# Mixer layer with 32 experts on one core: five expert weight loads ahead of the output projection instead of four, two buffers for normalized rows, gates times b2 at experts 6, 12, 18 and 24

## The chip, the core and the metric

The kernel runs on one core of one Trainium2 chip. The metric is the device time of one execution in microseconds (us). A core has five engines that run their own instruction queues: TensorE (PE in the rows; PEld is its weight load), VectorE (DVE), ScalarE (ACT), GpSimd (POOL) and SyncE (SP), whose queue here issues the weight loads. They wait for each other through semaphores. Transfers run on 16 DMA engines that all queues share.

## What is computed

One layer over 512 latent tokens of width 1024 (with 256 context tokens): an adaptive LayerNorm, one input projection whose columns feed a bidirectional RWKV-7 part and a Fourier part, one output projection, a residual with LayerNorm, then a mixture of experts and a second residual with LayerNorm. The change touches the seam between the output projection and the experts. Each token takes 4 of 32 experts; `gate` is the softmax over its four router logits. For the rows `u` of one expert `e`:

```
h   = u @ w1[e] + b1[e]            # 1024 -> 2 x 1024, two halves: linear and gated
act = clamped_swiglu(h)            # 1024
y   = act @ w2[e] + b2[e]          # 1024 -> 1024
out[token] += gate[token, e] * y   # scattered back, then the second residual and LayerNorm
```

The kernel adds the term `gate * b2` apart from the rest: for each group of 128 tokens, the matrix of gates (128 x 32) times `b2` (32 x 1024).

## The kernel before

**Output projection (L1553 to L1597).** Four tiles of 128 tokens go one after another. For each, TensorE makes the projection (L875, L914), VectorE takes mean and variance of it from PSUM (L1566, L1567) and writes the normalized rows to the tile `yo` (L1573); TensorE transposes them (L1578), ScalarE scales them (L1581), TensorE makes the router logits (L1584) and transposes back (L1591), VectorE adds the bias and takes the eight largest logits (L1585, L1586), ScalarE copies out the experts' input (L1592). GpSimd makes the residual from `yo` (L1595, L1596). The last L1586 is followed by the router (from L1627) and that by the experts. The rows that the projection reads are closed by a "finish" chain on VectorE, ScalarE and TensorE (L834, L836, L841, L844, L850, L852, L856, L857), once for each half of its columns.

**Expert constants.** Ahead of the four tiles in the program stand loads and preparations for the experts. The bias b1 comes in two tiles `b1r` of 1024 columns, which take the same tag `yo` and so the same buffers as the normalized rows. ScalarE makes a bf16 copy `b1s` (L1545), VectorE subtracts it (L1548), and ScalarE stores the rest as further bf16 parts (L1549). `b2r` is b2 times a modulation vector (L1551, GpSimd).

**Experts.** 32 experts, each with a fixed number of slots: 128, 32, 160, 32, 96, 64, 96, 192, 32, 64, 96, ... . The slots are cut into blocks of 64 and 32 rows. Expert i has 8 up slabs (w1) and 4 down slabs (w2), each a load of 1 MB on SP's queue (L1328, `raw<-in_w`), 384 loads in one stream, into 14 buffers: RAWA of them in a pool that is opened ahead of the projection, RAWB in one that is opened when the router's buffers are gone. A buffer comes free when TensorE has multiplied its slab with the expert's blocks (L1337). In step i of `all_experts` stand in this order: the slots of expert i+2 (one-hot products L1249, gather L1305), the up products of expert i (L1337, closed by the bias product L1344 with `sel`, which GpSimd casts at L1300), the transposes of the activations of expert i-1 (L1389) and of the rows of expert i+1 (L1316), the down products of expert i-1 (L1337 on `at`), VectorE's product with the gate (L1408) and the accumulate into DRAM (L1414, an indirect transfer from GpSimd's queue). One-hot products, transposes and the product below write to `pt`, two PSUM buffers in all.

**Gates times b2.** `b2_part(j)` treats the j-th 128 tokens: four matmuls (L1479), two copies of PSUM to the tile `yb` by ScalarE (L1480; `yb` has one buffer), and one accumulate of 512 KB on GpSimd's queue (L1481). Before, it is called in steps 4, 5, 6 and 7.

A recording layer gathers all instructions and a scheduler sets the order on each engine, so that program order is only a preference; each engine then runs its row strictly in order.

Of the kernel before, what the change touches and what calls it, by code (L numbers as in the profile page):

```python
# [10 lines left out]
F32 = mybir.dt.float32  # L11
# [9 lines left out]
T, TC, D = 512, 256, 1024  # L21
# [123 lines left out]
def body(ctx, tc, I, out, dbg=None, stop=None):  # L145
# [944 lines left out]
    P = Pair()  # L1090
    P.po = po
    post = moe(tc, I, ck, h2d, accd, modd, P)
    next(post)
    pq = pool(sO[1], "pq", side="right")
# [30 lines left out]
    sK.close()  # L1125


RAWA, RAWB = 4, 10
LATE = ("y64", "y32", "act64", "act32", "at64", "at32", "sg", "slin", "sth")
FIRST = 200  # L1130
NBLK = 48
# [56 lines left out]
def moe(tc, I, ck, h2d, accd, modd, P):  # L1188
# [6 lines left out]
    def pool(stack, name, bufs=1, **kw):  # L1195
        return stack.enter_context(tc.tile_pool(name=name, bufs=bufs, reuse_waits="tile", **kw))
# [269 lines left out]
    def place(i):  # L1466
        j, cap = PLAN[i]
        return Expert(cap, rm[:, :, j], R6[:, :, j], sel3[:, j:j + 1])

    def chosen(i):  # L1470
        j = PLAN[i][0]
        return SY.value_load(eidi[0:1, j:j + 1], min_val=0, max_val=NE - 1)

    def b2_part(j):

        y = B.tile([128, D], F32, "yb", 1)
        for n in range(2):
            p = pst.tile([128, 512], F32, name="pt", tag="pt")
            PE.matmul(p, gwT[:, j * 128:(j + 1) * 128], b2r[:, n * 512:(n + 1) * 512], start=True, stop=True)  # L1479
            A.activation(y[:, n * 512:(n + 1) * 512], p, AF.Copy)  # L1480
        G.indirect_dma_start(out=accd[:, :], out_offset=bass.IndirectOffsetOnAxis(ap=toki[:, j:j + 1], axis=0),  # L1481
                             in_=y, in_offset=None, compute_op=ALU.add)

    def all_experts():
        cur, prev = first, None
        ahead = [place(i) for i in range(1, len(PLAN))]
        yield cur.split
        yield ahead[0].fetch
        for i in range(len(PLAN)):
            nxt = ahead[i] if i + 1 < len(PLAN) else None  # L1490
            if i + 2 < len(PLAN):
                yield ahead[i + 1].fetch
            ups = list(cur.up())
            yield from ups[:8 if nxt else 4]
            if nxt:
                nxt.weights(chosen(i + 1))
            if prev:
                yield prev.turn
            if nxt:
                yield nxt.split  # L1500
            if prev:
                yield from prev.down()
                yield prev.put
                if 4 <= i < 8:
                    yield lambda j=i - 4: b2_part(j)
            if not nxt:
                yield from ups[4:]
            prev, cur = cur, nxt
        yield prev.turn
        yield from prev.down()  # L1510
        yield prev.put
# [4 lines left out]
    po = pool(so, "pl", side="left")  # L1516
# [9 lines left out]
    B = Buffers(None, 99, (praw, RAWA))  # L1526
    first = Expert(PLAN[0][1], rm0, R60, M["sel0"][0:96]).weights(0)
    experts = Run(all_experts())
    experts.load(RAWA)
    sb_ = ExitStack()  # L1530
# [8 lines left out]
            SY.dma_start(z[n * h:n * h + n], row_bcast(modd, 8 * n, 3072 + 8 * n * h, n))  # L1539
    for n in range(2):  # L1540
        c = slice(n * D, (n + 1) * D)
        b1r = po.tile([128, D], F32, name="yo", bufs=3)
        for h in range(3):
            SY.dma_start(b1r[32 * h:32 * h + 32], I["b1"][0][:, c])
        A.activation(b1s[:, c], b1r[0:96], AF.Copy)  # L1545
        for h in (1, 2, 2):
            q = slice(32 * h, 32 * h + 32)
            V.tensor_tensor(b1r[q], b1r[q], b1s[q, c], op=ALU.subtract)  # L1548
            A.activation(b1s[q, c], b1r[q], AF.Copy)  # L1549
# [5 lines left out]
    for j in P.order:  # L1555
        tk = slice(j * 128, (j + 1) * 128)
        p = mixer(j)
        if "y" in dbg:
            y = po.tile([128, D], F32, name="yd")
            for hh in range(2):  # L1560
                A.activation(y[:, hh * 512:(hh + 1) * 512], p[hh], AF.Copy)
            SY.dma_start(dbg["y"][tk, :], y)
        st = po.tile([128, 2, 6], F32, name="sto", bufs=2)
        mv = po.tile([128, 2], F32, name="mvo", bufs=2)
        for hh in range(2):
            V.bn_stats(st[:, hh, :], p[hh])  # L1566
        V.bn_aggr(mv, st)  # L1567
        rs = po.tile([128, 1], F32, name="rso", bufs=2)
        A.activation(rs, mv[:, 1:2], AF.Sqrt, bias=epsl, scale=1.0)
        V.reciprocal(rs, rs)  # L1570
        y = po.tile([128, D], F32, name="yo", bufs=3)
        for hh in range(2):
            V.tensor_scalar(y[:, hh * 512:(hh + 1) * 512], p[hh], mv[:, 0:1], rs, op0=ALU.subtract, op1=ALU.mult)  # L1573
        h2T = po.tile([128, KD, 128], F32, name="h2T", bufs=2)
        for q in range(2):
            pt = pst.tile([128, 4, 128], F32, name="pt")
            for z in range(4):
                PE.transpose(pt[:, z], y[:, (4 * q + z) * 128:(4 * q + z + 1) * 128], ident)  # L1578
            for z in range(4):
                k = 4 * q + z  # L1580
                A.activation(h2T[:, k], pt[:, z], AF.Identity, bias=B2c[:, k:k + 1], scale=G2c[:, k:k + 1])  # L1581
        pl = psl.tile([128, NE], F32, name="pl")
        for k in range(KD):
            PE.matmul(pl, h2T[:, k], wrt[:, k], start=(k == 0), stop=(k == KD - 1))  # L1584
        V.tensor_tensor(lg[:, j], pl, brt, op=ALU.add)  # L1585
        V.max(mx[:, j], lg[:, j])  # L1586
        h2 = po.tile([128, D], F32, name="h2o", bufs=2)
        for q in range(2):
            pt = pst.tile([128, 4, 128], F32, name="pt")
            for z in range(4):  # L1590
                PE.transpose(pt[:, z], h2T[:, 4 * q + z], ident)  # L1591
            A.activation(h2[:, q * 512:(q + 1) * 512], pt.rearrange("p z c -> p (z c)"), AF.Copy)  # L1592
        SY.dma_start(h2d[tk, :], h2)
        x = po.tile([128, D], F32, name="xo", bufs=2)
        G.tensor_tensor(x, y, ag, op=ALU.mult)  # L1595
        G.tensor_tensor(x, x, ab, op=ALU.add)  # L1596
        SY.dma_start(accd[tk, :], x)  # L1597
# [250 lines left out]
```

## Time and profile before

| | before |
|---|---|
| median of 3 runs | 1820.64 us (1817.49 to 1822.31) |
| profiled execution, its own time | 1815.8 us |
| its span in the profile | 1813.8 us |
| mean granted TensorE clock | 0.929 of full |
| TensorE busy | 1612.2 us (89%) |
| VectorE / ScalarE / GpSimd busy | 755.1 / 392.6 / 431.3 us |
| bytes moved | 572.72 MB, mean 316 GB/s |
| of these the SP queue's | 520.11 MB |

Spans and times of instructions are those of the profiled execution. In rows of a timeline, the first number is the start in us from the span's beginning and the second the time that the group took; the bracket at the end is the idle time of the engine just before it and what ended it. A group of equal instructions that follow each other stands in one row (x is their number). Times of POOL are rough. In rows of windows stand the window, its length, the busy us (and number of instructions) of PE, PEld, DVE, ACT and POOL, the granted TensorE clock as a share of full, the mean busy share of the DMA engines and GB/s. The experts' stage lasts from about 700 us to about 1780 us.

### The profile page before, as it was taken

The page shows a single profiled execution, that of the slowest core. Times are in us where ns is not written, and L with a number is a line of the kernel's source. Part 1 is how long each engine was busy: PE and PEld are TensorE (multiplying, and loading weights), DVE is VectorE, ACT ScalarE, POOL GpSimd, SP SyncE. Part 2 cuts the span into 40 slices and gives each one's busy share as a digit, 9 for nine tenths or more (in the row PEclk, how much of TensorE's full clock was granted, in tenths as well). Part 3 has the DMA queues.
Part 4 walks back from the last instruction along what each step waited for, and adds up shares of the span by engine and source line. Part 5 has one row for each costly group of instructions (what it writes and reads, how often), then busy time and mean ns, then how long its engine had stood idle before and what let it go on. Part 6 is the DMA issues. An engine that isn't in the chain of part 4 may idle for free. (4 is left out here: it accounts for less than half of the span.)

```text
span 1813.8 us, 38967 instructions
## 1 busy us (share of the span) xinstructions
PE 1612.2 (89%) x16148; PEld 875.3 (48%) x16148; DVE 755.1 (42%) x1775; ACT 392.6 (22%) x771; POOL 431.3 (24%) x436
## 2 busy tenths in 40 slices
PE   4889887677999977999959999999999999989982
PEld 1767655566787863454413453443244344324430
DVE  4899977887446674222111121231112211211113
ACT  3565465232223250110010000100000100001002
POOL 1444434264134341101020211111111100112112
PEclk9899888786899977999979999999999999999995
DMA  8567859675575538999996999999899999999995
GB/s 320 168 198 255 252 175 282 182 219 151 174 245 184 201 125 317 414 381 405 416 315 203 386 405 408 412 414 416 340 398 401 411 414 419 408 412 400 402 406 197
DMA packets 205508, 572.72 MB, mean 316 GB/s; under 512 B 28449, under 2 KB 116129, under 8 KB 156177
## 3 DMA queue, kind: packets, MB, share of 16 engines
q1 hardware_dynamic: 144624, 520.11, 73.9%
q0 software_dynamic: 11840, 24.91, 5.9%
q10 hardware_dynamic: 48864, 25.17, 4.8%
q8 instruction: 129, 2.11, 0.5%
q14 instruction: 51, 0.41, 0.1%
HBM read 512.57 MB, written 57.56 MB: 314 GB/s over the span
## 5 line engine op out<-in xcount | busy, mean ns | idle before, releaser
L1337 PE MATMUL st<-raw,xt 128*32 128x512 f32 (+1 forms) x6784 | 634.7, 525 | 18.9 <-DMA raw<-in_w 13.0
L1337 PEld LDWEIGHTS st<-raw,xt 128*32 128x32 f32 x6784 | 244.3, 110 | 368.8 <-issue 285.1
L1337 PE MATMUL st<-raw,at 128*32 128x512 f32 (+1 forms) x3392 | 319.3, 521 | 6.9 <-ACT at L1391 3.1
L1371 DVE TENSOR_SCALAR sg<-st 128x256 f32<-128x256 f32 x87 | 36.4, 419 | 511.5 <-PE st L1344 511.5
L1337 PEld LDWEIGHTS st<-raw,at 128*32 128x32 f32 x3392 | 111.0, 111 | 187.9 <-issue 148.6
L1372 ACT ACTIVATE sth<-sg 128x256 f32<-128x256 f32 x87 | 36.1, 415 | 719.4 <-DVE sg L1371 693.5
L1414 POOL DMA_INDIRECT accd<-y,idx x53 | 86.3, 1628 | 292.6 <-DVE y L1408 145.3
L1408 DVE SCALAR_TENSOR_TENSOR y<-st,gt,gt2h 128x512 f32<-128x512 f32 (+1 forms) x53 | 34.7, 655 | 249.0 <-PE st L1337 215.7
L1305 POOL DMA_INDIRECT xg<-h2d,idx x53 | 53.2, 1004 | 247.7 <-DVE idx L1270 228.4
L1300 POOL CAST sel<-sel 96x64 bf16<-96x64 f32 x31 | 9.2, 298 | 395.3 <-PE st L1344 376.4
L328 PE MATMUL pj<-hhi,wh 128*128 128x512 f32 (+1 forms) x240 | 90.0, 377 | 9.8 <-DVE hlo L281 9.8
L328 PE MATMUL pj<-hhi,wl 128*128 128x512 f32 (+1 forms) x240 | 90.9, 380 | 8.8 <-DVE wl L324 8.8
L328 PE MATMUL pj<-hlo,wh 128*128 128x512 f32 (+1 forms) x240 | 90.9, 379 | 0.0
L652 PE MATMUL big<-Rb,Lt 128*128 128x256 f32 (+1 forms) x192 | 51.9, 420 | 13.4 <-DVE pk L658 5.0
L1391 ACT ACTIVATE at<-pt 128x512 f32<-128x512 f32 (+1 forms) x53 | 26.8, 518 | 143.3 <-PE pt L1389 143.0
L328 PEld LDWEIGHTS pj<-hhi,wl 128*128 128x128 f32 x240 | 47.7, 199 | 20.2 <-DVE wl L324 11.0
L328 PEld LDWEIGHTS pj<-hhi,wh 128*128 128x128 f32 x240 | 47.4, 197 | 19.6 <-DVE hlo L281 10.1
L752 POOL TENSOR_TENSOR SW<-S,Wc 64x128 f32<-64x128 f32 (+1 forms) x66 | 31.3, 475 | 96.4 <-DVE S L787 76.8
L328 PEld LDWEIGHTS pj<-hlo,wh 128*128 128x128 f32 x240 | 47.5, 198 | 13.8 <-issue 7.2
L407 DVE SCALAR_TENSOR_TENSOR acc<-war,sil,acc 128x512 f32<-128x512 f32 x56 | 52.8, 943 | 0.8 <-ACT acc L404 0.6
L1318 ACT ACTIVATE xt<-pt 128x512 f32<-128x512 f32 (+1 forms) x53 | 27.0, 518 | 99.2 <-PE pt L1316 98.7
L652 PEld LDWEIGHTS big<-Rb,Lt 128*128 128x128 f32 x192 | 37.0, 230 | 20.8 <-issue 10.2
(390 smaller groups left out, 2249.3 us busy)
## 6 DMA issues: line engine op xcount, KB each, us to landing
raw<-in_w SPq DMA_DIRECT2D x384, 1024.0 KB
war<-in_w_ada SPq DMA_DIRECT2D x64, 256.0 KB
chd<-pk ACTq DMA_DIRECT2D x52, 256.0 KB
wr<-in_w_in ACTq DMA_DIRECT2D x40, 256.0 KB
wa<-in_w_ada SPq DMA_DIRECT2D x16, 512.0 KB
win<-chd SPq DMA_DIRECT2D x8, 896.0 KB
win<-chd SPq DMA_DIRECT2D x16, 448.0 KB
ltd<-Lt SPq DMA_DIRECT2D x8, 768.0 KB
```

The source lines that it names most:

```text
L328: PE.matmul(p, a[:, k, :], b[:, k0 + k, t0:t0 + n], start=(k0 + k == 0 and i == 0), stop=(k0 + k == KD - 1 and i == 2))
L407: V.scalar_tensor_tensor(acc, wr, sil0[:, k:k + 1], acc, op0=ALU.mult, op1=ALU.add)
L652: PE.matmul(ps[:, z], Lu[:, u0 + (z0 + z if d == 0 else 3 - z0 - z), :], Rb[:, z0 + z], start=True, stop=True)
L752: G.tensor_tensor(SW[HALF[p]].rearrange("p z d c -> p (z d) c"), S[HALF[p], :, :, p].rearrange("p z d c -> p (z d) c"), Wc[HALF[p], 2 * c0 ...
L1305: G.indirect_dma_start(out=x, out_offset=None, in_=h2h[n], in_offset=bass.IndirectOffsetOnAxis(ap=idx[:, 0:1], axis=0))
L1318: A.activation(xt.rearrange("p k s -> p (k s)"), p, AF.Copy)
L1337: PE.matmul(r, x(s * slices + b, o), c(raw[:, b * 2048 // slices:(b + 1) * 2048 // slices]), start=(s + b == 0 and first), stop=(s == n - ...
L1371: V.tensor_scalar(g, u2[:, :, 0], 7.0, None, op0=ALU.min)
L1372: A.activation(t, g, AF.Tanh, scale=0.851)
L1391: A.activation(at.rearrange("p k s -> p (k s)"), p, AF.Copy)
L1408: V.scalar_tensor_tensor(y, st, gt, gt2h[n], op0=ALU.mult, op1=ALU.mult)
L1414: G.indirect_dma_start(out=acch[n], out_offset=bass.IndirectOffsetOnAxis(ap=idx[:, 0:1], axis=0), in_=y, in_offset=None, compute_op=ALU.add)
```

## The change

The first pool of weight buffers gets five buffers instead of four and the second nine instead of ten, so five loads are issued ahead of the projection. The tag `yo` has two buffers instead of three. The four calls of `b2_part` move from steps 4 to 7 to steps 6, 12, 18 and 24.

```diff
-RAWA, RAWB = 4, 10
+RAWA, RAWB = 5, 9
...
             if prev:
                 yield from prev.down()
                 yield prev.put
-                if 4 <= i < 8:
-                    yield lambda j=i - 4: b2_part(j)
+                if i in (6, 12, 18, 24):
+                    yield lambda j=i // 6 - 1: b2_part(j)
...
-        b1r = po.tile([128, D], F32, name="yo", bufs=3)
+        b1r = po.tile([128, D], F32, name="yo", bufs=2)
...
-        y = po.tile([128, D], F32, name="yo", bufs=3)
+        y = po.tile([128, D], F32, name="yo", bufs=2)
```

On VectorE, in the output projection, the order before had the first two tiles' normalized rows (`yo_6503`, `yo_6578`) ahead of the split of b1 (L1548 on `yo_6395` and `yo_6406`), and the last finish chain's L852 and L857 among the splits:

```order
L1573 TENSOR_SCALAR yo_6578<-pm_6562,mvo_6571,rso_6575 128x512
L850 SCALAR_TENSOR_TENSOR Ys_3486<-Ys_3486,cols_73,w_6469 128x2x128 x2
L1585 TENSOR_TENSOR lg_5423<-pl_6525,brt_5438 128x32
L1548 TENSOR_TENSOR yo_6395<-yo_6395,b1s_6382 32x1024 x2
L852 TENSOR_TENSOR Ys_3486<-Ys_3486 128x2x128
L1586 MAX mx_5433<-lg_5423 128x8
L1548 TENSOR_TENSOR yo_6406<-yo_6406,b1s_6382 32x1024 x2
```

In the order of the changed kernel the finish chain is through first, then all of the split, then the first tile's rows (`yo_6505`):

```order
L850 SCALAR_TENSOR_TENSOR Ys_3486<-Ys_3486,cols_73,w_6471 128x2x128 x2
L852 TENSOR_TENSOR Ys_3486<-Ys_3486 128x2x128
L857 TENSOR_TENSOR mxlg1_6034<-Ys_3486,mxhg1_6033 128x2x128
L1548 TENSOR_TENSOR yo_6397<-yo_6397,b1s_6384 32x1024 x2
L1548 TENSOR_TENSOR yo_6408<-yo_6408,b1s_6384 32x1024 x2
L1548 TENSOR_TENSOR yo_6397<-yo_6397,b1s_6384 32x1024
L1548 TENSOR_TENSOR yo_6408<-yo_6408,b1s_6384 32x1024
L1573 TENSOR_SCALAR yo_6505<-pm_6481,mvo_6498,rso_6502 128x512
```

The first rows tile thus stands behind six L1548 instead of ahead of them, and L857 ahead of them instead of behind five.

On GpSimd, around experts 6 and 7, the order before was this; `sel` are the casts for the bias product, `xg` the gathers, `y64`, `y32` and `yb` the sources of accumulates:

```order
L1300 CAST sel_9033<-sel3_5427 96x64
L1414 DMA accd_78<-y32_8678,idx_7452 2560x256
L1300 CAST sel_9343<-sel3_5427 96x64
L1481 DMA accd_78<-yb_8683,toki_5432 640x1024
L1414 DMA accd_78<-y64_8991,idx_7703 1280x512
L1414 DMA accd_78<-y32_8993,idx_7728 2560x256
L1305 DMA xg32_9035<-h2d_77,idx_9030 128x256
L1481 DMA accd_78<-yb_8999,toki_5432 640x1024
```

In the changed kernel the same place holds no accumulate of `yb`, and the first one comes two casts later:

```order
L1300 CAST sel_9017<-sel3_5427 96x64
L1414 DMA accd_78<-y32_8678,idx_7452 2560x256
L1305 DMA xg32_9019<-h2d_77,idx_9014 128x256
L1300 CAST sel_9327<-sel3_5427 96x64
L1414 DMA accd_78<-y64_8983,idx_7703 1280x512
L1305 DMA xg64_9329<-h2d_77,idx_9324 128x512
L1414 DMA accd_78<-y32_8985,idx_7728 2560x256
L1300 CAST sel_9781<-sel3_5427 96x64
L1414 DMA accd_78<-y64_9288,idx_8107 1280x512
L1481 DMA accd_78<-yb_9293,toki_5432 640x1024
```

The first two accumulates of `yb` that stood here (`yb_8683`, `yb_8999`) are gone from the place, and the first of the changed kernel is behind the cast for expert 10.

Further on in the changed kernel, on the same engine, stand the second accumulate of `yb` and those of expert 12 (`y64_11540`, `y64_11542`, `y32_11544`), with the cast for expert 19 (`sel_12501`) among them:

```order
L1481 DMA accd_78<-yb_11258,toki_5432 640x1024
L1305 DMA xg64_11943<-h2d_77,idx_11888 128x512
L1414 DMA accd_78<-y64_11540,idx_10272 1280x512
L1414 DMA accd_78<-y64_11542,idx_10297 1280x512
L1305 DMA xg64_11945<-h2d_77,idx_11913 128x512
L1300 CAST sel_12501<-sel3_5427 96x64
L1414 DMA accd_78<-y32_11544,idx_10322 2560x256
L1305 DMA xg64_11947<-h2d_77,idx_11938 128x512
L1414 DMA accd_78<-y32_11860,idx_10616 2560x256
```

The accumulate of `y32_11544` is behind the cast for expert 19, and `yb_11258` is new here.

## Rows read from the trace of the kernel before

**Rows 1.** 20-us windows, experts: busy us of PE, PEld, DVE, ACT, POOL; clock; DMA.

```profile
900.00:920.00 20.00, 8.23 (x112) 3.40 (x105) 4.20 (x12) 1.66 (x4) 1.81 (x2) 0.76 1.02 394
...
940.00:960.00 20.00, 13.48 (x120) 3.68 (x123) 1.33 (x6) 1.09 (x2) 5.61 (x4) 0.74 0.72 168
960.00:980.00 20.00, 20.00 (x192) 5.55 (x188) 0.00 (x0) 0.00 (x0) 0.00 (x0) 1.00 0.57 208
980.00:1000.00 20.00, 19.53 (x214) 7.75 (x210) 8.09 (x24) 3.62 (x9) 0.23 (x1) 1.00 0.55 202
...
1020.00:1040.00 20.00, 20.00 (x202) 6.63 (x198) 3.49 (x9) 0.00 (x0) 4.15 (x3) 1.00 1.02 391
```

**Rows 2.** TensorE's waits, 700 to 1790 us: total, times, longest.

```profile
PE pt L1249 <- ACT yb L1480: 20.5, 2, 12.0
PE st L1337 <- DMA raw<-in_w: 15.9, 21, 1.9
```

**Rows 3.** TensorE's timeline, experts 6 and 7.

```profile
886.33 21.24 PE L1337 MATMUL st<-raw,xt 128*32 128x512 f32 x256
...
920.24 0.28 PE L1249 MATMUL pt<-R,O 128*32 128x6 bf16 x16 [12.01 <-ACT yb L1480]
...
932.45 1.98 PE L1479 MATMUL pt<-b2r,gwT 32*128 32x512 f32 x4
...
946.52 0.28 PE L1249 MATMUL pt<-R,O 128*32 128x6 bf16 x16 [8.54 <-ACT yb L1480]
946.63 40.37 PE L1337 MATMUL st<-raw,xt 128*32 128x512 f32 x352
```

**Rows 4.** ScalarE's timeline, the same stretch.

```profile
919.59 1.09 ACT L1480 ACTIVATE yb<-pt 128x512 f32<-128x512 f32 x2 [8.51 <-DMA accd<-yb,toki]
```

**Rows 5.** GpSimd's timeline, the same stretch.

```profile
908.39 0.23 POOL L1300 CAST sel<-sel 96x64 bf16<-96x64 f32 x1 [35.26 <-PE st L1344]
909.17 1.58 POOL L1481 DMA_INDIRECT accd<-yb,toki  x1 [0.54 <-ACT sth L1372]
...
1021.87 1.59 POOL L1481 DMA_INDIRECT accd<-yb,toki  x1 [6.11 <-DMA accd<-y,idx]
```

**Rows 6.** 10-us windows, columns as in rows 1: the projection, the first experts.

```profile
660.00:670.00 10.00, 9.08 (x32) 7.19 (x33) 5.45 (x10) 7.44 (x14) 2.12 (x1) 0.50 0.13 52
...
700.00:710.00 10.00, 10.00 (x84) 2.63 (x80) 0.00 (x0) 0.00 (x0) 0.00 (x0) 0.88 0.85 353
710.00:720.00 10.00, 10.00 (x139) 3.30 (x135) 3.86 (x16) 0.60 (x1) 1.89 (x2) 1.00 0.26 87
```

**Rows 7.** VectorE's timeline, output projection.

```profile
635.91 1.52 DVE L1573 TENSOR_SCALAR yo<-pm,mvo,rso 128x512 f32<-128x512 f32 x2
...
645.08 1.52 DVE L1573 TENSOR_SCALAR yo<-pm,mvo,rso 128x512 f32<-128x512 f32 x2
...
647.51 5.93 DVE L1548 TENSOR_TENSOR yo<-yo,b1s 32x1024 f32<-32x1024 f32 x2
...
659.88 1.22 DVE L1548 TENSOR_TENSOR yo<-yo,b1s 32x1024 f32<-32x1024 f32 x1
661.12 0.42 DVE L857 TENSOR_TENSOR mxlg<-Ys,mxhg 128x256 fp32r<-128x256 f32 x1
...
674.61 0.81 DVE L1573 TENSOR_SCALAR yo<-pm,mvo,rso 128x512 f32<-128x512 f32 x1
...
679.86 0.20 DVE L1586 MAX8 mx<-lg 128x8 f32<-128x32 f32 x1
```

**Rows 8.** ScalarE's timeline, output projection.

```profile
643.93 1.04 ACT L1545 ACTIVATE b1s<-yo 96x1024 bf16<-96x1024 f32 x1
...
676.23 2.90 ACT L1581 ACTIVATE h2T<-pt,gbc 128x128 f32<-128x128 f32 x8 [0.38 <-PE pt L1578]
```

**Rows 9.** GpSimd's timeline, output projection.

```profile
649.02 3.33 POOL L1551 TENSOR_TENSOR b2r<-b2r,gt 32x1024 f32<-32x1024 f32 x1
```

**Rows 10.** TensorE's timeline, output projection.

```profile
656.42 0.80 PE L875 MATMUL pm<-woh,mxhg 128*128 128x512 f32 x1 [4.50 <-ACT mxhg L856]
```

## Prediction

> **What bounds the kernel now.** I read the 20-us windows of the expert stage first, then the list of TensorE's waits there, then the timelines of TensorE, ScalarE and GpSimd around the longest of them, and last the timelines of the output projection.
>
> In the windows the reader is to see two things that run nearly full side by side. DMA stands at a share of 1.02 and about 400 GB/s (390 to 410), so a load of 1.05 MB takes some 2.5 us (an estimate: 1.05 MB by 410 GB/s), and TensorE is busy for all 20 us, as in 1020 to 1040 [rows 1]. So the end of the stage moves with what both lose, and both lose it in one place, 900 to 1000 us. TensorE is idle first: in 900 to 920 it works 8.2 of 20 us, while DMA still runs full, because not all of the 14 weight buffers are taken yet. Then DMA is idle: 0.72, 0.57 and 0.55 in the three windows from 940, together 20 x (0.30 + 0.45 + 0.47) / 1.02 = 23.9 us of lost transfer time.
>
> The waits name the cause: 20.5 us are two waits for `yb`, more than the 15.9 us of all 21 waits for weights [rows 2]. The timeline places them: 12.01 us before 920.24 and 8.54 us before 946.52, each ahead of the one-hot products, which share the two `pt` buffers with the gates' product L1479 [rows 3]. ScalarE in turn could not write `yb` (one buffer) until the accumulate of the round before had left it [rows 4], and that one was issued only at 909.17, behind a cast on GpSimd that waited 35.26 us for expert 6's bias product [rows 5]. After the second wait comes expert 7, with 192 rows: 352 matmuls in 40.37 us, at 48 a slab 5.5 us for each [rows 3], twice what DMA needs for one. While it runs, each load waits for the slab that it replaces. The 24 us that DMA loses are this: TensorE entered its longest expert late, and the loads had nowhere to go.
>
> **The change part by part.** *The waits for `yb` go.* The four rounds now follow the down products of experts 5, 11, 17 and 23, six experts apart; 32 experts share some 1080 us (700 to 1780), so that is 200 us, and no write of `yb` meets an accumulate under way, however late GpSimd sends it. Saved on TensorE: 12.01 + 8.54 = 20.5 us. *The products are moved.* L1479 takes 1.98 us a round [rows 3]; all four rounds are still made. Of three ahead of expert 7's up products one stays: 2 x 1.98 = 4.0 us less there, paid later. TensorE thus enters expert 7 up to 24.5 us earlier, at 910 instead of 932.45 + 1.98 = 934.4. Its weights allow nearly that: DMA ran full while TensorE stood [rows 1], and built up a lead.
>
> *What DMA makes of it.* Expert 7 still takes 5.5 us a slab against 2.5, so some idle time remains. In the trace its up products end at 946.63 + 40.37 = 987 [rows 3], and with some 5 us for the last transfer the eight loads that replace its slabs end near 992. With 24.5 us less they end near 968. The stream runs full until near 940 in both (its share falls in that window), so the 28 us from 940 to 968 hold eight loads, 20 us, and 8 us stay idle; with the edges of that stretch 6 to 13 of the 23.9. All transfers are still made, so the stream gains what it no longer idles: 23.9 - 6 = 18 us, 11 at worst.
>
> *What the moved accumulates cost.* One moves 0.5 MB, 1.3 us at 410 GB/s. The window 940 to 960 suggests more: its 168 GB/s are 8.2 us of a full DMA, its share of 0.72 is 14.1, and about three accumulates lie in it (one of `y`, one of `yb`, and a `yb` begun just before 940), so 5.9 / 3 = 2.0 more for each. Between 1.3 and 3.3 I take 2.2. Two of the four lay in idle stretches before; now three stand where DMA is full (experts 12, 18, 24), and one that stood in a full window (1021.87 [rows 5]) is gone: 2 x 2.2 = 4.4 us. Counted forward, the stream leads by 24.5 us behind expert 7 and gives back 4.4: 20. TensorE's own ledger says 20.5, waits gone and no work gone. Between 18 and 20.5 I take **-19 us** for the experts, with -11 and -24.5 as bounds.
>
> *The fifth early load.* There are 14 buffers before and after, and all 14 loads have landed before the fifteenth is issued: DMA's share is 0.85 in 700 to 710 and 0.26 in 710 to 720, and TensorE is busy for 10 of 10 us in both [rows 6]. The fifteenth waits until TensorE frees its first slab, late, because block 0 of expert 0 passes over all eight slabs before block 1. Worth **0** (2.5 us, one load, if TensorE were short there).
>
> *Two row tiles instead of three.* The two b1 tiles of L1542 and the four normalized rows of L1571 share the tag `yo`. With three buffers the first rows were written at 635.91, before b1 was split [rows 7]. With two they wait until a b1 tile is split, and VectorE has all six L1548 ahead of them. The b1 loads stand behind five raw loads instead of four, 2.5 us. ScalarE's first L1545 ends at 643.93 + 1.04 = 644.97 [rows 8], so near 647.5 after, which is when L1548 began before. Six of them last 6 x 1.22 = 7.3 us alone; beside GpSimd's L1595, L1551 and L1596 two took 5.93 us, 2.97 each [rows 7, 9]. Of those three only L1551 (3.33 us, so two of the six) still falls beside them, as no rows exist yet for the others: 4 x 1.22 + 2 x 2.97 = 10.8 us at most. That puts the first L1573 at 655 to 658, some 20 us later than before. [...]
>
> In exchange the finish chain, whose last link L857 at 661.12 stood between the splits [rows 7] and kept TensorE waiting 4.50 us at 656.42 [rows 10], is done ahead of them, some 20 us earlier, so the projection's products lie ready. From 656 on four tiles follow each other. The last one took from 674.61 to 679.86 + 0.20, 5.4 us. Between the starts of two lie at least ScalarE's 2.90 us for L1581, some 4 with its two L1592 [rows 8], and at most what lay between the first two before, 645.08 - 635.91 = 9.2 us [rows 7]. So the last L1586 ends at 656 + 3 x (4 to 9.2) + 5.4 = 673 to 689, against 680.06. [...]
>
> **Sum.** -19 + 5 + 0 = -14 us. The profiled execution took 1815.8 us (span 1813.8), so 1801.8. The median of the runs shown is 1820.64, 4.8 above it; on that footing 1806.6, say **1807**. What can be told from no change is 0.3%, 5.5 us.
>
> **The rivals.** *A: the gain stays hidden (about 1818; 0.13).* DMA idles under expert 7 anyway, because that expert is long: 13 us remain, the accumulates cost 3.3 us each (2 x 1.1 more), and the projection takes its +7: -11 + 2 + 7 = -2. For it: both are near full, so what one saves shows as a wait for the other. Against: both lost in the same 100 us, and both get it back.
>
> *B: the projection is not late (about 1801; 0.13).* The finish chain's 20 us make up for the late first tile, 0, and 19 to 20 remain. For it: the last tile hung on L857 and not on `yo`. Against: four tiles in a row from 656.
>
> *C: the projection takes most of it (about 1817; 0.10).* Each tile waits for its buffer, as the third for GpSimd's L1595 of the first, and TensorE stays at the lower clock, as at 0.50 behind the wait at 656.42 [rows 6, 10]: a tile takes 10 us, 656 + 4 x 10 = 696, +16; -19 + 16 = -3. [...]
>
> *D: a new wait in GpSimd's queue (slower, about 1828; 0.08).* In the new order the cast for expert 19 stands ahead of the accumulate of expert 12's `y32` and waits for expert 16's bias product. `y32` has two buffers, so VectorE's L1408 for expert 14 waits for that accumulate, and behind it TensorE for a free `st`. It is the mechanism of the wait that goes, at another place. If it lasts as long as the up products of a 96-row expert, 21.24 us (at 886.33 [rows 3]), it is 1807 + 21; it decides the sign from 14 us on. Against: the order of before has the same crossing, and its long waits are others [rows 2].
>
> My own sum keeps 0.56, with 1798 to 1813 as its range. It and B are faster, and of A, C and D a fifth, on their lucky side: 0.75. Same 0.16 (A and C, the rest), slower 0.09. The range 1796 to 1820 leaves out D, the far end of C and of B.
>
> **What would show it.** Right: no wait of TensorE for L1480; expert 7's run of L1337 starting 15 to 20 us earlier; two of the three windows that stood at 0.55 to 0.72 at 0.8 or more; the rounds of L1479 some 200 us apart; the last L1586 near 685. Wrong: the last L1586 past 690 (C) or at 680 (B); waits for L1408 or `accd` on TensorE or VectorE (D); shares of 0.6 again under expert 7 (A). Most likely to break the forecast is the projection, whose term rests on a clock level that I can't foresee.

## Result and profile after

The changed kernel takes 1807.11 us (median of 3 runs, 1806.30 to 1807.86) against 1820.64: a ratio of 0.9925, with a 95% interval from 0.9909 to 0.9942. That is 13.5 us faster, and the forecast was 1807. Behind the total stand terms that were not all of the size forecast; the experiments show which, though not the cause of each.

Spans of single executions mislead here. Up to the load of the LayerNorm rows (L1522), which stands ahead of all that the change moves, TensorE's and VectorE's rows are the same in both kernels, and yet that load is issued at 617.5 us in the profile of before and at 621.1 in this one; in the other twelve profiles below it lies between 619.8 and 624.2. The profiled execution of before was the quickest of all fourteen up to there. So the stages are compared from that load on:

| us | before | changed | difference |
|---|---|---|---|
| up to the issue of L1522 | 617.5 | 621.1 | +3.6, scatter |
| from there to the experts' first L1337 | 82.1 | 87.2 | +5.1 |
| first to last L1337 | 1083.5 | 1062.5 | -21.0 |
| tail, to the end | 30.7 | 33.6 | +2.9 |

The last three give -13.0, which agrees with the timed runs.

The list of TensorE's waits, 690 to 1790 us, with total, times and longest:

```profile
PE st L1337 <- DMA raw<-in_w: 13.3, 15, 1.6
PE pt L1316 <- DMA xg<-h2d,idx: 11.0, 3, 5.6
PE st L1337 <- ACT xt L1318: 3.6, 5, 1.1
```

The two waits for `yb` [rows 2] are gone, and those for weights are no longer than before. Of the three waits for a gather the first stood before too, just ahead of the window of rows 2, at the start of the experts. Before:

```profile
697.68 1.11 PE L1316 MATMUL pt<-mcst,xg 128*128 128x128 f32 x4 [2.24 <-DMA xg<-h2d,idx]
```

and now, with the two that are new further on:

```profile
706.33 1.11 PE L1316 MATMUL pt<-mcst,xg 128*128 128x128 f32 x4 [4.25 <-DMA xg<-h2d,idx]
...
1251.09 0.63 PE L1316 MATMUL pt<-mcst,xg 128*128 128x128 f32 x4 [1.14 <-DMA xg<-h2d,idx]
...
1266.89 1.09 PE L1316 MATMUL pt<-mcst,xg 128*128 128x128 f32 x4 [5.60 <-DMA xg<-h2d,idx]
```

TensorE's timeline around experts 6 and 7:

```profile
922.72 1.98 PE L1479 MATMUL pt<-b2r,gwT 32*128 32x512 f32 x4
...
928.19 38.31 PE L1337 MATMUL st<-raw,xt 128*32 128x512 f32 x352
```

One round of products stands ahead of expert 7, with no wait behind it. Its 352 matmuls take 38.31 us and not 40.37 [rows 3]. The reason stands in the windows (columns as in rows 1), where the clock is 1.00, and was 0.76 and 0.74 in the windows of the two waits [rows 1]:

```profile
900.00:920.00 20.00, 19.75 (x225) 10.70 (x220) 4.27 (x12) 3.26 (x7) 1.84 (x2) 1.00 1.02 410
920.00:940.00 20.00, 20.00 (x182) 7.13 (x178) 2.08 (x7) 1.19 (x2) 2.57 (x2) 1.00 1.03 409
940.00:960.00 20.00, 20.00 (x192) 7.96 (x188) 0.00 (x0) 0.00 (x0) 0.00 (x0) 1.00 1.01 422
960.00:980.00 20.00, 19.53 (x216) 8.73 (x212) 8.09 (x24) 3.62 (x9) 3.74 (x3) 1.00 0.72 238
980.00:1000.00 20.00, 19.79 (x277) 11.53 (x271) 5.41 (x18) 2.58 (x5) 3.85 (x4) 1.00 1.03 375
...
1260.00:1280.00 20.00, 14.40 (x117) 4.16 (x112) 1.48 (x4) 0.60 (x1) 5.20 (x4) 0.83 1.03 397
```

Of the 23.9 us that DMA lost here, one window is left, 20 x 0.30 / 1.02 = 5.9 us. The last row shows TensorE idle for 5.6 us at a place where it was not before, the wait at 1266.89. GpSimd's timeline around it:

```profile
1244.49 1.59 POOL L1414 DMA_INDIRECT accd<-y,idx  x1 [0.31 <-issue]
1254.91 1.57 POOL L1414 DMA_INDIRECT accd<-y,idx  x1 [8.83 <-DMA accd<-y,idx]
1256.78 1.01 POOL L1305 DMA_INDIRECT xg<-h2d,idx  x1 [0.30 <-DVE act L1375]
1257.79 0.25 POOL L1300 CAST sel<-sel 96x64 bf16<-96x64 f32 x1
1264.80 1.59 POOL L1414 DMA_INDIRECT accd<-y,idx  x1 [6.75 <-DMA accd<-y,idx]
1266.69 1.02 POOL L1305 DMA_INDIRECT xg<-h2d,idx  x1 [0.30 <-issue]
1274.05 1.57 POOL L1414 DMA_INDIRECT accd<-y,idx  x1 [6.35 <-DMA accd<-y,idx]
1275.93 1.02 POOL L1305 DMA_INDIRECT xg<-h2d,idx  x1 [0.30 <-issue]
```

The accumulates, which all add into one tensor, wait for each other, and the gathers for later experts stand behind them in the queue: the gather that TensorE waited for is the one issued at 1256.78, behind an accumulate that had waited 8.83 us.

VectorE's timeline in the output projection answers to rows 7:

```profile
644.53 0.43 DVE L857 TENSOR_TENSOR mxlg<-Ys,mxhg 128x256 fp32r<-128x256 f32 x1 [0.48 <-ACT mxhg L856]
647.75 9.33 DVE L1548 TENSOR_TENSOR yo<-yo,b1s 32x1024 f32<-32x1024 f32 x6 [2.79 <-ACT b1s L1545]
657.10 1.53 DVE L1573 TENSOR_SCALAR yo<-pm,mvo,rso 128x512 f32<-128x512 f32 x2
...
687.36 0.20 DVE L1586 MAX8 mx<-lg 128x8 f32<-128x32 f32 x1
```

and TensorE's the length of its gap:

```profile
657.97 1.12 PE L1578 MATMUL pt<-mcst,yo 128*128 128x128 f32 x4 [15.92 <-DVE yo L1573]
```

The finish chain is through at 645, the six splits follow as one block, and only then come the first rows; TensorE waits 15.92 us for them. With the 3.6 us of scatter taken off, the last L1586 ends at 684.0 instead of 680.06. The clock was at 0.50 only at the beginning of the four tiles, until near 663, as the windows show:

```profile
650.00:660.00 10.00, 2.03 (x7) 1.51 (x7) 8.54 (x7) 6.40 (x9) 2.39 (x2) 0.50 0.01 2
660.00:670.00 10.00, 10.00 (x48) 7.47 (x48) 3.69 (x8) 3.51 (x9) 5.96 (x4) 0.84 0.13 52
670.00:680.00 10.00, 9.75 (x60) 7.75 (x59) 6.10 (x13) 5.09 (x14) 7.26 (x4) 1.00 0.28 117
```

### The profile page after: what moved, and what is told of

The parts are those of the page before. It is cut to its first block, busy times and chain, and to the rows that moved or that the text cites. A ratio compares the mean times of both kernels' runs of the same rounds, so it can differ in the third digit from the quotient of the medians.

```text
span 1804.4 us, 38970 instructions
## 1 busy us (share of the span) xinstructions
PE 1603.2 (89%) x16148; PEld 887.1 (49%) x16148; DVE 746.9 (41%) x1775; ACT 391.7 (22%) x771; POOL 427.5 (24%) x436
## 5 line engine op out<-in xcount | busy, mean ns | idle before, releaser
L1337 PE MATMUL st<-raw,xt 128*32 128x512 f32 (+1 forms) x6784 | 632.4, 522 | 14.7 <-DMA raw<-in_w 9.7
L1337 PEld LDWEIGHTS st<-raw,xt 128*32 128x32 f32 x6784 | 259.8, 110 | 346.7 <-issue 276.0
L1337 PE MATMUL st<-raw,at 128*32 128x512 f32 (+1 forms) x3392 | 320.1, 520 | 6.6 <-DMA raw<-in_w 3.6
L1337 PEld LDWEIGHTS st<-raw,at 128*32 128x32 f32 x3392 | 113.1, 110 | 186.9 <-issue 148.1
L1372 ACT ACTIVATE sth<-sg 128x256 f32<-128x256 f32 x87 | 36.2, 416 | 671.7 <-DVE sg L1371 671.7
L1408 DVE SCALAR_TENSOR_TENSOR y<-st,gt,gt2h 128x512 f32<-128x512 f32 (+1 forms) x53 | 34.7, 654 | 236.0 <-PE st L1337 210.0
```

The costliest lines, as they stand in the source:

```text
L1337: PE.matmul(r, x(s * slices + b, o), c(raw[:, b * 2048 // slices:(b + 1) * 2048 // slices]), start=(s + b == 0 and first), stop=(s == n - ...
L1372: A.activation(t, g, AF.Tanh, scale=0.851)
L1408: V.scalar_tensor_tensor(y, st, gt, gt2h[n], op0=ALU.mult, op1=ALU.mult)
```

## Experiments

The times of each kernel and of the kernel before were taken on the same chip; the ratios are what can be compared between kernels. The traces are one execution each. "Start", "experts" and "tail" are the last three stages of the table above, as differences to the profile of before. "Lead" is how much earlier the n-th L1337 of the experts begins than in the profile of before, both counted from the first (worked out from the records of both traces).

| kernel | ratio (95% interval) | start | experts | tail |
|---|---|---|---|---|
| changed | 0.9925 (0.9909 to 0.9942) | +5.1 | -21.0 | +2.9 |
| moved calls alone | 0.9868 (0.9851 to 0.9885) | -0.9 | -24.0 | +0.2 |
| two `yo` buffers alone | 1.0030 (1.0018 to 1.0042) | +2.6 | +2.0 | +1.0 |
| five early loads and two `yo` buffers | 1.0046 (1.0025 to 1.0067) | +4.8 | +0.6 | 0.0 |
| two `yb` buffers alone | 0.9961 (0.9946 to 0.9975) | +0.3 | -13.7 | +8.2 |
| b1 in a buffer of its own | 0.9995 (0.9983 to 1.0008) | +4.3 | -5.7 | +0.2 |
| moved calls, no accumulate of `yb` | 0.9869 (0.9849 to 0.9889) | -0.6 | -27.9 | +5.9 |
| moved calls, three early loads | 0.9868 (0.9849 to 0.9886) | -2.3 | -22.4 | -0.6 |
| calls at 6, 11, 19, 24 | 0.9878 (0.9858 to 0.9898) | -2.1 | -20.4 | 0.0 |
| moved calls and two `yo` buffers | 0.9952 (0.9934 to 0.9971) | +2.5 | -16.5 | +5.7 |
| changed, calls at 6, 11, 19, 24 | 0.9918 (0.9892 to 0.9945) | +4.2 | -18.2 | -0.1 |
| changed, six accumulates less | 0.9918 (0.9886 to 0.9950) | +4.8 | -27.9 | +7.8 |
| before, six accumulates less | 0.9946 (0.9927 to 0.9965) | -0.7 | -9.3 | -1.3 |

**The parts by themselves.** The moved calls alone, on the kernel before:

```diff
-                if 4 <= i < 8:
-                    yield lambda j=i - 4: b2_part(j)
+                if i in (6, 12, 18, 24):
+                    yield lambda j=i // 6 - 1: b2_part(j)
```

> The kernel before with the four calls of b2_part at experts 6, 12, 18 and 24 alone; four early loads and three yo buffers stay. Theory: the waits for yb are worth 18 to 19 us in the experts and the later projection costs 5, so without the projection's part this kernel is faster than before by 18 to 19 us, about 1802, and its last L1586 ends near 680 plus the offset of its execution. Rival (the projection's delay is only scatter between executions): about 1807, as the changed kernel. Rival (the gain comes from the fifth early load): about 1820.

Measured: 1797.34 us, beside 1820.83 for before. The first theory names the right place and is some 5 us short; both rivals are out. This kernel is faster than before and than the changed one: it is the version to keep.

Two `yo` buffers alone:

```diff
-        b1r = po.tile([128, D], F32, name="yo", bufs=3)
+        b1r = po.tile([128, D], F32, name="yo", bufs=2)
...
-        y = po.tile([128, D], F32, name="yo", bufs=3)
+        y = po.tile([128, D], F32, name="yo", bufs=2)
```

> The kernel before with two yo buffers instead of three, and nothing else. Theory: the first normalized rows wait for the split of b1, the last L1586 ends 4 us later, and the kernel is 4 to 5 us slower than before, about 1825; the 20.5 us of waits for yb stay. Rival (the finish chain, which is through earlier, makes up for it): within 1 us of before.

Measured: 1827.22 us, beside 1820.83; the interval is 3.3 to 7.6 us slower. The theory's size holds in the time. The trace puts less of it in the projection than the theory's 4 us: the last L1586 ends 64.1 us behind L1522 instead of 62.6, 1.5 us later, the experts begin 2.6 us later, and another 3.0 us lie in the experts and the tail. The waits for `yb` are there unchanged, 20.6 us in its list.

The changed kernel with the calls put back:

```diff
-                if i in (6, 12, 18, 24):
-                    yield lambda j=i // 6 - 1: b2_part(j)
+                if 4 <= i < 8:
+                    yield lambda j=i - 4: b2_part(j)
```

> The changed kernel with the calls of b2_part back at experts 4 to 7, so five early loads and two yo buffers alone. Theory: the fifth load is worth 0 and the two buffers cost 4 to 5 us: about 1825, the same as two yo buffers alone. Rival (the fifth load gives back a load's 2.5 us): about 1822. The 20.5 us of waits for yb are there in both.

Measured: 1828.36 us, from runs that spread from 1822.36 to 1847.85. Its interval and that of two `yo` buffers alone overlap, so the fifth load's own share is not told apart by the times. In the traces the first L1573 comes 36.2 us behind L1522 instead of 33.7, which is a load's time later, and the start is 2.2 us later. Without the moved calls the fifth load gives nothing back that shows.

**Wait or place.** Two `yb` buffers in the kernel before, calls at 4 to 7:

```diff
-        y = B.tile([128, D], F32, "yb", 1)
+        y = B.tile([128, D], F32, "yb", 2)
```

> The kernel before with two yb buffers instead of one; the calls of b2_part stay at experts 4 to 7. Theory: what counted was the wait of the pt buffers for yb, not where the products stand, so this gives the same 18 to 20 us, about 1801 to 1803, with waits for L1480 near 0. Rival (the place counts: four accumulates and 8 us of products ahead of the 192-row expert keep TensorE late): half of it or less, 1811 or more.

Measured: 1814.40 us, a third of the gain: the rival's number, but not by the rival's reason. In expert 7 (the 2300th L1337) its lead is 24.6 us, as the end of the waits alone should give with the clock: 20.5 us of waits, and from the 1500th to the 2500th L1337 TensorE's matmuls cover 111.0 us instead of 115.2 (the products have not moved here). It is given back later, to 13.8 at the 5000th and, after 22.3 at the 7000th, to 13.9 at the last. Its list has 20.9 us of waits for weights instead of 15.9; what gives the rest back is not shown. More is lost in the tail, where GpSimd's timeline shows four accumulates that follow each other at the end, the last two behind the last L1337:

```profile
1762.46 1.55 POOL L1414 DMA_INDIRECT accd<-y,idx  x1 [24.07 <-DVE y L1408]
1771.41 1.55 POOL L1414 DMA_INDIRECT accd<-y,idx  x1 [7.39 <-DMA accd<-y,idx]
1776.24 1.55 POOL L1414 DMA_INDIRECT accd<-y,idx  x1 [3.29 <-issue]
1781.71 1.55 POOL L1414 DMA_INDIRECT accd<-y,idx  x1 [3.91 <-DMA accd<-y,idx]
```

**Why the projection is late.** The same memory, split otherwise: two `yo` buffers for the rows, one for b1, on the kernel before:

```diff
-        b1r = po.tile([128, D], F32, name="yo", bufs=3)
+        b1r = po.tile([128, D], F32, name="b1r", bufs=1)
...
-        y = po.tile([128, D], F32, name="yo", bufs=3)
+        y = po.tile([128, D], F32, name="yo", bufs=2)
```

> The kernel before with two yo buffers for the normalized rows and one buffer of its own for the b1 tiles (the same memory as three yo buffers); the calls of b2_part stay at experts 4 to 7. Theory: what costs in the changed kernel is that the first normalized rows wait for the split of b1, not that there are two buffers; here the first L1573 stands ahead of the L1548 again, so it comes some 18 us behind L1522 as before, the projection is as long as before within 1 us, and the time is that of before, about 1821. Rival (two buffers for four tiles are too few): the third rows wait for the first tile's last reader and the time is 1825 or more, as with two yo buffers alone.

Measured: 1818.80 us, beside 1819.58: no difference that can be told. VectorE writes the first rows ahead of the splits again:

```profile
637.03 1.53 DVE L1573 TENSOR_SCALAR yo<-pm,mvo,rso 128x512 f32<-128x512 f32 x2
...
651.43 6.08 DVE L1548 TENSOR_TENSOR b1r<-b1r,b1s 32x1024 f32<-32x1024 f32 x2 [0.22 <-issue]
```

and the last L1586 ends 61.5 us behind L1522, 1.1 earlier than before. So the projection's delay comes from the shared tag and not from the number of buffers for rows. In this one profile the experts start 4.3 us later all the same, since TensorE waits 8.22 us for the first gather, and make it good by shorter waits for `yb` (14.2 us). So the equal time shows less by itself than the trace of the projection does: without the waits for `yb`, such a late start might cost something.

**What the moved accumulates cost.** The moved calls without the accumulate:

```diff
-        G.indirect_dma_start(out=accd[:, :], out_offset=bass.IndirectOffsetOnAxis(ap=toki[:, j:j + 1], axis=0),
-                             in_=y, in_offset=None, compute_op=ALU.add)
```

> The kernel before with b2_part at experts 6, 12, 18 and 24, without the accumulate L1481: the products L1479 and the copies L1480 stay, gates times b2 is not added to the output. Theory A (the moved accumulates cost the stream 2.2 us each where DMA is full): 6 to 9 us faster than with them, about 1790. Theory B (TensorE bounds the experts with 1026 us of work in 1059, and an accumulate costs only where a gather stands behind it on GpSimd's queue): 0 to 3 us faster, about 1795.

Measured: 1796.24 us, a ratio of 0.9869 against 0.9868 with the accumulate. Theory B holds for the time, within the some 5 us that the intervals leave. The traces are not so plain: without the four accumulates the waits for weights are 9.6 us instead of 16.1 and the experts take 3.9 us less, which is theory A's direction, and the tail takes 5.7 us more. There, accumulates of the last experts are still waiting for each other when the last L1337 has ended, at 1758.9:

```profile
1749.98 1.55 POOL L1414 DMA_INDIRECT accd<-y,idx  x1 [8.60 <-DMA accd<-y,idx]
1760.39 1.55 POOL L1414 DMA_INDIRECT accd<-y,idx  x1 [8.86 <-DVEq L1758]
1765.37 1.55 POOL L1414 DMA_INDIRECT accd<-y,idx  x1 [3.43 <-DMA accd<-y,idx]
```

**The early load.** The moved calls with one early load less:

```diff
-RAWA, RAWB = 4, 10
+RAWA, RAWB = 3, 11
```

> The kernel before with b2_part at experts 6, 12, 18 and 24, and three early loads with eleven later ones instead of four and ten. Theory: all 14 loads have landed before TensorE frees the first slab, so an early load more or less is worth nothing for the experts; the b1 loads come one load earlier, but VectorE has other work then: within 2 us of four early loads, about 1797. Rival (an early load is worth its 2.5 us of transfer): about 1800.

Measured: 1795.22 us, the ratio of four early loads. So three are as good as four where `yo` is left alone, as far as intervals of 3 to 4 us to either side can tell; the rival's 2.5 us are less than they resolve. No run has five with `yo` left alone.

**Another place.** The moved calls at other steps, on the kernel before and on the changed one:

```diff
-                if i in (6, 12, 18, 24):
-                    yield lambda j=i // 6 - 1: b2_part(j)
+                if i in (6, 11, 19, 24):
+                    yield lambda j=(6, 11, 19, 24).index(i): b2_part(j)
```

> The kernel before with b2_part at experts 6, 11, 19 and 24 instead of 6, 12, 18 and 24, four early loads and three yo buffers. Experts 12 and 17 have 160 and 192 rows; in the changed kernel the second round stood behind expert 12's products and its accumulate ahead of a chain of accumulates and gathers near 1220 to 1300 us. Theory: the place matters by the few us that a gather waits there (1.9 us with four early loads), so 1794 to 1798. Rival: any place that is six experts apart is alike, and another order elsewhere costs as much: 1797 to 1800.

Measured: 1796.05 us.

> The changed kernel with b2_part at experts 6, 11, 19 and 24 instead of 6, 12, 18 and 24. Theory: the 5.60 us for which TensorE waits for a gather at 1266.89 in the changed kernel hang on the chain of accumulates there, and not on the round at expert 12 alone; with four early loads the same move left 5.0 us of such a wait and changed the time by no more than 1 us: so within 2 us of the changed kernel, 1805 to 1809. Rival (that wait is the round at expert 12): 5 us less, about 1802.

Measured: 1806.43 us. Neither differs from 6, 12, 18 and 24, and a wait of 5.0 us for a gather is found in both: it does not hang on the round at expert 12. Behind the first gather, calls at 6, 11, 19, 24 have 6.7 us of such waits, as much as the changed kernel, and the moved calls alone 1.9 us, and yet their times are not told apart. So these waits by themselves cost little in the end. The two kernels of this section have the same order of accumulates and gathers on GpSimd, and differ by the fifth load and the two `yo` buffers: 0.9878 against 0.9918, some 7 us (1 to 13), of which the traces have 6.3 us at the start and 2.2 in the experts.

**Do the parts add?** The moved calls with two `yo` buffers and four early loads:

```diff
-        b1r = po.tile([128, D], F32, name="yo", bufs=3)
+        b1r = po.tile([128, D], F32, name="yo", bufs=2)
...
-        y = po.tile([128, D], F32, name="yo", bufs=3)
+        y = po.tile([128, D], F32, name="yo", bufs=2)
```

> The kernel before with b2_part at experts 6, 12, 18 and 24 and two yo buffers shared by b1 and the normalized rows; four early loads. Theory: the parts add, so 5.5 to 6.4 us (two yo buffers alone) above the 1797 of the moved calls alone: about 1803, and the rest to the changed kernel's 1807 belongs to the fifth early load, which puts the b1 loads one load later. Rival (the fifth load costs nothing and two yo buffers cost the whole): 1806 to 1808.

Measured: 1812.38 us, slower than both numbers expected. It is also slower than the changed kernel by the ratios, but the two intervals touch. The parts do not add: the ratios of the parts give 0.9898, the kernel has 0.9952. The start is as in two `yo` buffers alone (+2.5); what is missing lies in the experts (-16.5) and the tail (+5.7).

**The chain of accumulates.** From the 5200th L1337 (near 1232 us in the changed kernel) to the 5600th (near 1285) its lead falls from 26.5 to 14.3 us. The accumulates of that stretch were left out, in the changed kernel and, as a control, in the one before:

```diff
-                yield prev.put
+                if i not in (13, 14, 15):
+                    yield prev.put
```

> The changed kernel without the accumulates L1414 of experts 12, 13 and 14, so that their rows don't reach the output (six of 53 accumulates). In the changed kernel TensorE's lead over the kernel before shrinks from 29 to 14 us between 1230 and 1290 us, while seven accumulates follow each other on GpSimd's queue, each waiting for the one before. Theory (this chain holds the gathers and so TensorE): without it the lead stays above 22 us there, no wait of TensorE for a gather near 1267, and the kernel is 6 to 10 us faster than the changed one, about 1797 to 1801. Rival (the lead shrinks because DMA can't bring the weights faster): the lead shrinks as before and the time is 1803 to 1807, the 3 MB of transfers less being worth 2 to 4 us.

> The kernel before without the accumulates L1414 of experts 12, 13 and 14, as the control of the same cut in the changed kernel. Theory (the chain counts only when TensorE is ahead): within 3 us of before, 1817 to 1821. Rival (the accumulates cost the stream wherever they stand): as much faster as in the changed kernel, 6 us or more.

Measured: 1805.91 and 1809.88 us. At its place the theory holds: the lead is 26.3 at the 5600th, 35.2 at the 6000th, and no wait for a gather is listed from 1220 to 1300. Its time fails. The rival's time is met and its lead is not, so neither is right as a whole; the difference to the changed kernel is 1 us, give or take 7. In the trace the experts are 6.8 us shorter than in the changed kernel, and the tail takes 4.9 of them back: 38.5 us instead of 33.6, with accumulates at 1758.69, 1767.11, 1771.56 and 1776.58, the last three behind the last L1337. On the way the lead falls once more, from 31.9 at the 7600th to 19.5 at the 8000th, and is 29.8 again at the 9000th. TensorE waits there for a gather,

```profile
1519.09 0.66 PE L1316 MATMUL pt<-mcst,xg 128*128 128x128 f32 x2 [6.67 <-DMA xg<-h2d,idx]
```

but for another reason than a chain of accumulates. GpSimd's last accumulate stood 25 us earlier, and the gather waited for the indices of its rows, which VectorE computes (L1270):

```profile
1490.07 1.56 POOL L1414 DMA_INDIRECT accd<-y,idx  x1 [8.18 <-DMA accd<-y,idx]
1515.39 1.01 POOL L1305 DMA_INDIRECT xg<-h2d,idx  x1 [23.77 <-DVE idx L1270]
```

VectorE made them at 1514.92, behind work on an expert whose bias product (L1344) had kept it waiting 15.78 us, until 1512.24. The control gained 9.5 us, more than the theory's 3 and for the rival's reason or another: it lost most of its waits for weights (5.0 us instead of 15.9) and kept those for `yb`.

## Why the prediction came out right, step by step

**The waits and their cause: right.** The 20.5 us of waits for `yb` are gone, and the moved calls alone carry the whole gain. The step that sized it fell short. I took -19 between 18 and 20.5, since I expected the stream of weights to give part of it back; the waits for weights did not grow (15.9 before, 13.3 after, 16.1 with the moved calls alone). What I left out is the clock. In windows of 0.5 us of the profile of before it stood at 0.50 from near 911 to 924 and from near 941 to 951.5, so for some 4 and 5 us behind the ends of the two waits (920.24 and 946.52). At the place itself this is clear in all profiles: from the 1500th to the 2500th L1337 of the experts, the L1337 alone cover 101.5 to 102.3 us in the five kernels that have the waits, and 97.7 in the eight that have the calls moved (worked out from the records), some 4 us. Over the whole stage the moved calls alone have 1026.4 us of matmuls instead of 1030.0 and 20.4 us less of idle time, together the 24.0 that they save; but between other kernels that sum varies as much for other reasons, from 1023.7 to 1032.7. In windows of 20 us the clock is 0.76 and 0.74 around the waits and 1.00 without them.

**What DMA makes of it: right as a picture, needless as a ledger.** The idle time left under expert 7 was put at 6 to 13 us; 5.9 are left, so the stream gained 18. But TensorE's waits and clock alone gave the moved calls 24.0, more than that, so the stream was not what set the time here.

**What the moved accumulates cost: not found in the time.** The sum had 4.4 us for it. The times show none (0.9869 without the accumulates, 0.9868 with them). In the traces the experts are 3.9 us shorter without them, and the tail takes it back.

**The fifth early load: right, as far as it was tried.** Three and four early loads are alike in time. In the projection the fifth put the first rows 2.5 us later (36.2 against 33.7 us behind L1522, with the calls left at 4 to 7), which the sum had.

**Two row tiles: right.** Forecast were the splits from 647.5 for 7.3 to 10.8 us, the first rows near 656, the last L1586 at 685, and 5 us. Measured, with the scatter off: splits from 644.2 for 9.33 (3.25 for the one beside GpSimd's L1551 and some 1.21 for each of the others), first rows at 653.5, last L1586 at 684.0, and 5.1 us at the experts' start. Of these 5.1, 3.9 are the projection's; 2.0 are a longer wait for the first gather (4.25 against 2.24), less 0.8 won in the router. No run shows the 5 us of the sum by itself: it was my estimate, in the upper half of 673 to 689 on account of the clock. In its place the runs showed a start that is later by 5.1 us in the changed kernel and by 2.6 with two `yo` buffers alone, and in the changed kernel a clock of 0.50 when the first tile began and of 1.00 for the other three. That the total of the projection was so near is in part luck: the first rows came 2.5 us earlier than forecast, and the last tile took 9.4 us (678.11 to 687.56) and not 5.4. That the projection is late because of the shared tag is shown by the run that gives b1 its own; that the whole cost in time comes from there is not, since the traces of two `yo` buffers alone have only 1.5 us of it in the projection.

**What the sum did not have.** Against the moved calls alone the changed kernel is 10.4 us slower by the ratios (6 to 15), and the sum had 5 of them. The traces have 6.0 at the start, 3.0 in the experts (-21.0 instead of -24.0) and 2.7 in the tail. The 5.7 us of the last two nearly cancel against the 5 us by which the moved calls were worth more than -19, and so -14 came out as -13.5. The total was right partly because two omissions had opposite signs.

Of the 3.0 us in the experts I can't name the cause. TensorE waits 6.7 us for two gathers, 5.6 of them for one behind accumulates that wait for each other, but its idle time in the stage is only 2.0 us longer than with the moved calls alone, and calls at 6, 11, 19, 24 have the same 6.7 us with no loss that the times tell. The tail is clearer. In all fourteen profiles 28.6 to 31.2 us pass from the start of the last accumulate to the end. That accumulate starts 0.83 us behind the end of the last L1337 in nine of them, 2.48 in the changed kernel, and 6.5 to 9.9 in the four whose tail is 5.7 to 8.2 us longer: there one or two other accumulates still have to go ahead of it when TensorE is done.

**The rivals.** A and C are out by the time. B is out too, though the finish chain was 20 us earlier with the scatter off, as it supposed: TensorE still had nothing to do until the first rows. D did not happen: TensorE's list shows no wait for L1408. The other sign that I had named for it, a wait of VectorE for an accumulate, did show in the changed kernel and in the moved calls alone, in this order:

```profile
DVE y L1408 <- DMA accd<-y,idx: 7.9, 1, 7.9
```

```profile
DVE y L1408 <- DMA accd<-y,idx: 8.9, 1, 8.9
```

The moved calls alone are among the fastest of all these kernels, so that sign by itself tells nothing of TensorE.

**The footing.** I set the median of before 4.8 us above the profiled execution and gave no reason. The profiles suggest one: that execution was 2.3 to 6.7 us ahead of all others at L1522.

**Open.** Why the moved calls with two `yo` buffers come out some 5 us above the changed kernel, which has one early load more, is not settled. 2.8 us lie in the tail, where two accumulates are left over instead of one. In the experts TensorE's idle time is the same (35.0 and 35.1 us), and its matmuls cover 1032.0 us instead of 1027.4; why, no run shows. I had thought of the order that the scheduler makes of accumulates and gathers, which differs between these two kernels. But it can't be all: two `yo` buffers alone have the same order as the kernel before and cost 5.5 us, and the two kernels with calls at 6, 11, 19, 24 share one order and differ by 7. The run without the chain's accumulates had no wait at that place and won no time that could be told.

## What to carry to other kernels

A single-buffered tile written by one engine and drained by an indirect transfer on another engine's queue can stop a third one through the PSUM buffers that they share; here its worth was the wait (20.5 us) plus the time at a lower clock behind it (0.50, some 4 us), and both stand in the trace. Before a buffer count is cut, look at who shares the tag: a tile of constants that was prepared late in the same ring delayed the first tile of the loop here (first rows at 653.5 instead of 635.91), and a buffer of its own in the same memory cost nothing that could be told (0.9995). Where accumulates into one tensor follow each other, time that is won ahead of them may be lost again in the tail (which was longer by 5.7 to 8.2 us in four kernels here), so look how many are left when the last product is done; and measure each part of a change by itself before all of it.

## What the runs showed of the hardware

An accumulate of 64 or 32 rows (256 or 128 KB) into one DRAM tensor took long beside the weight stream: a median of 9.2 us from issue to landing, in the profile of before as in that of the changed kernel, and in the chain of the latter from 1244.49 to 1274.05 each starts 9.3 to 10.4 us after the one that it waits for. Four accumulates of `yb` fewer (2 MB) changed no time that could be told, and six of `y` fewer none in the changed kernel, but 9.5 us in the kernel before. In these three cases TensorE's waits for weights became shorter, by 6.5, 4.0 and 10.9 us. And two executions of the same instructions differ by 2 to 7 us within their first 620 us, as much as half the effect studied here.
